# Passing both halves of the transposed probabilities through one value product per key block, in a one-core decoder layer

## Chip, core and metric

One core of one Trainium2 chip runs the whole program. The metric is the device time of one launch in microseconds (us). Five engines matter here: TensorE (PE in the profile; PEld is its weight load), VectorE (DVE), ScalarE (ACT), GpSimd (POOL) and SyncE (SP), which only issues transfers. Each engine takes its instructions strictly in the order of its own queue.

## What is computed

One layer of a decoder trunk on 256 tokens of width 1024, in float32. Three attention mixers run side by side, their outputs are merged by gates, and two layer norms with a feed-forward part follow. Cut to what matters:

```python
proj = x @ w_in                        # queries, keys, values of all three mixers
o_a = dsa_mixer(...)                   # 6 heads, top-64 keys of a learned index, one shared k and v
o_b = dilated_mixer(...)               # 4 slots x 3 window patterns
o_c = moba_mixer(...)                  # 6 heads
...
# in every mixer, at the end:
probs = masked_softmax(logits, mask)
out = jnp.einsum('bqhk,bqkd->bqhd', probs.astype(v.dtype), vsel)
...
merged = (gates[:, :, 0] * (o_a @ w_br_a) + gates[:, :, 1] * (o_b @ w_br_b)
          + gates[:, :, 2] * (o_c @ w_br_c))
x = layer_norm(ALPHA * x + merged @ w_out, ln1_g, ln1_b)
h = jnp.square(jax.nn.relu(x @ w_up)) @ w_down
ple = jax.nn.sigmoid(x @ w_ple_gate) * (p @ w_ple)
x = layer_norm(ALPHA * x + h + ple, ln2_g, ln2_b)
```

With 256 tokens every window and block fits in the sequence, so each mixer becomes dense causal attention with its own mask. The three patterns of a slot of the second mixer share one set of probabilities after they are added up, so 16 times in the program (4 slots, 6 heads of the third mixer, 6 of the first) a 256 x 256 lower triangular matrix of probabilities P is multiplied by 256 x 64 values V.

## The kernel before

Every float32 number that goes into a matrix product is split into a high part that TensorE reads exactly and a low part, the rest. A product of two such numbers then takes three passes, high by high, high by low and low by high (`prod`, L127 to L129), added up in PSUM.

Weights stream in units of up to 128 x 1024 (`Weights`): SP issues the load (L66), ACT writes the high part `whi` (L70), DVE writes the first columns of the low part `wlo` and GpSimd the last ones (L74; of 1024 columns DVE takes 640 and GpSimd 384, of which each column block of 128 belongs to one step of a sum over the width of x). There are five buffers each of the raw weights and of both parts, and a unit's buffers come free only when TensorE, DVE and GpSimd are through with it. Most units feed `gemm`: 24 products of 256 columns, eight blocks of the width times three passes, into one of three PSUM banks named `mm`.

Between these weight products stand the heads. For a head, `logits` (L264) makes the scores into PSUM, DVE adds a bias table T and finds row maxima (L334, L350), ACT takes the exponential (L337, L359) and scales the rows (L326), and `attend` does the rest. P is held as 128 rows by 384 columns: columns 0 to 127 are the first 128 queries by the first 128 keys, columns 128 to 383 are the other 128 queries by all 256 keys. The quarter with early queries and late keys is zero and isn't held.

`attend` transposes the three 128 x 128 pieces on TensorE into the PSUM bank b3 (L303 to L305). ACT copies them as the high part `pth` (L306) and DVE subtracts to get the low part `ptl` (L307). Both are 512 columns wide with a block of 128 zeros in front, set once at the start (L185), so that the late keys can be multiplied over all 256 queries. Four products of 256 columns follow into bank b4 (L310 to L313): the values of each key block by the high and by the low part. The stationary operand holds 64 columns of the values' high part and 64 of their low part, so the upper 64 rows of the result must still be added to the lower 64: ACT copies them down (L315), and DVE adds (L316). For two heads together `pair_out` splits the result (L319, L320) into `op`, which the branch products read later.

In the second mixer (`slots`) GpSimd adds up the three patterns (L361, L362) between the exponential and the scaling. For the first mixer GpSimd also adds the top-k mask `am` to the bias tables well ahead of use (L490, L491, tile `ta`); the tables T come from device memory in three transfers each (L175), since a small product (L374), copied by ACT and written out to `tabd`, makes them at the start.

What the order within each queue is isn't written out: a scheduler with its own model of time orders the instructions of all engines when the program is built, and `tc.high_priority` only moves some of them ahead. So every edit can shift rows far from it.

Of the kernel before, what the change touches and what calls it, by code (L numbers as in the profile page):

```python
# [11 lines left out]
F32 = mybir.dt.float32  # L12
F32R = mybir.dt.float32r
ALU = mybir.AluOpType
# [6 lines left out]
S = 256  # L21
# [67 lines left out]
def hybrid_layer(ctx: ExitStack, tc: tile.TileContext, x0, xn, pT, wqk, wva, wvb, wg, wbc, wba,  # L89
                 wout, wup, wdn, wpg, wple, lnrow, rel, onehot, pick, out):  # L90
    nc = tc.nc
    pe, act, dve, pool = nc.tensor, nc.scalar, nc.vector, nc.gpsimd
# [10 lines left out]
    def turns(ids):  # L103

        while True:
            for i in ids:
                yield banks.tile([128, 512], F32, name=f"b{i}", tag=f"b{i}")

    ps_s, ps_t, ps_v, ps_a = turns((0, 1, 2)), turns((3,)), turns((4,)), turns((0, 1, 3, 2, 4))

    ident = keep.tile([128, 128], F32, name="ident")
# [9 lines left out]
    t = banks.tile([128, 512], F32, name="b4", tag="b4")  # L121
# [22 lines left out]
    p1, k1, kp = (right(n, b) for n, b in (("p1", 1), ("k1", 2), ("kp", 3)))  # L144
# [34 lines left out]
        return t  # L179


    pth = [p1.tile([128, 512], F32R, name=f"pth{i}") for i in range(2)]
    ptl = [p1.tile([128, 512], F32R, name=f"ptl{i}") for i in range(2)]
    for t in pth + ptl:
        pool.memset(t[:, 0:128].bitcast(F32), 0.0)  # L185

    idx = p1.tile([128, 384], F32, name="idx")
    am = p1.tile([128, 384], F32, name="am")
# [81 lines left out]
    V = p1.tile([128, 2, 11, 128], F32R, name="V")  # L270
    iw = p1.tile([128, 2, 8], F32, name="iw")
    op = pm.tile([128, 8, 2, S], F32R, name="op")
# [23 lines left out]
    n_pt = [0]  # L296

    def attend(P, vh, o, h):

        hi, lo = pth[n_pt[0] % 2], ptl[n_pt[0] % 2]  # L300
        n_pt[0] += 1
        t = next(ps_t)
        pe.transpose(t[:, 0:128], P[:, 256:384], ident)  # L303
        pe.transpose(t[:, 128:256], P[:, 0:128], ident)
        pe.transpose(t[:, 256:384], P[:, 128:256], ident)  # L305
        act.copy(hi[:, 128:512], t[:, 0:384])  # L306
        dve.tensor_tensor(lo[:, 128:512], t[:, 0:384], hi[:, 128:512].bitcast(F32),  # L307
                          op=ALU.subtract)
        v = next(ps_v)
        pe.matmul(v[:, 0:S], lhsT=V[:, 0, vh], rhs=hi[:, 256:512], start=True, stop=False)  # L310
        pe.matmul(v[:, 0:S], lhsT=V[:, 0, vh], rhs=lo[:, 256:512], start=False, stop=False)
        pe.matmul(v[:, 0:S], lhsT=V[:, 1, vh], rhs=hi[:, 0:256], start=False, stop=False)
        pe.matmul(v[:, 0:S], lhsT=V[:, 1, vh], rhs=lo[:, 0:256], start=False, stop=True)  # L313
        x = wk2.tile([64, S], F32, name="ov", tag="ov")
        act.copy(x, v[64:128, 0:S])  # L315
        dve.tensor_tensor(o[64 * h:64 * h + 64], v[0:64, 0:S], x, op=ALU.add)  # L316

    def pair_out(o, kt):
        act.copy(op[:, kt, 0], o)  # L319
# [61 lines left out]
    with ExitStack() as begin:  # L381
# [4 lines left out]
        with tc.high_priority(offset=1000):  # L386
# [4 lines left out]
            for k in range(KT):  # L391
                act.copy(xh[:, k], g0[:, k, 0:S])
                for a, b in cut[k]:
                    a = max(a, S)
# [4 lines left out]
        for k in range(KT):  # L399
            for i, (w, x) in enumerate(((sh, xh), (sh, xl), (sl, xh))):  # L400
                for f in range(FIRST):
                    pe.matmul(first[f], lhsT=w[:, k, 128 * f:128 * f + 128], rhs=x[:, k],  # L402
                              start=k == i == 0, stop=k == KT - 1 and i == 2)
        iq = [q_pair(ps, 0.125) for ps in first]
    tp, wk, wk2, sm = (right(n, b) for n, b in (("tp", 3), ("wk", 3), ("wk2", 2), ("sm", 6)))
# [12 lines left out]
    for j in range(4):  # L418
        s = logits(iq[j], kI)
# [21 lines left out]
    def opair():  # L441
        return wk2.tile([128, S], F32, name="o", tag="o")

    for j in range(2):
# [8 lines left out]
        o = opair()  # L453
# [10 lines left out]
    for j in range(3):  # L464
# [3 lines left out]
        s = logits(q, k)  # L468
        o = opair()
# [11 lines left out]
    for j in range(3):  # L481
        q = q_pair(feat(19 + j))
        s = logits(q, kA)
        o = opair()
# [146 lines left out]
    for b in range(2):  # L631
        t = slice(b * 128, (b + 1) * 128)
# [31 lines left out]
    for f in range(32):  # L664
        ps = mmbank(512).rearrange("p (b a t) -> p b a t", b=2, a=2)
        hi, lo = W.get(u_up[f][0])
# [3 lines left out]
        for k in range(KT):  # L670
            pe.matmul(ps[:, :, 0], lhsT=lo[:, cs[k]], rhs=x1[:, :, k, 0], start=False,  # L671
                      stop=k == KT - 1)
# [131 lines left out]
```

## Time and profile before

| what | value |
|---|---|
| runs of the kernel before | 452.64 us median of 3 (451.95 to 453.76) |
| the profiled execution, its time | 451.62 us |
| its span, first to last instruction | 449.8 us |
| granted TensorE clock, mean | 0.996 |
| PE busy | 97% of the span, 2935 products |
| DVE, ACT, POOL busy | 68%, 58%, 23% |
| the stage with the heads | about 17 to 212 us of the span |
| L310 to L313, 16 each | 306, 287, 281, 281 ns mean |

A product's row tells its start and a length that includes the way through the array, so rows of products overlap: the distance from one start to the next is what a product costs the queue. In a timeline row a bracket gives the engine's idle time just before it and what ended it. The profiled execution took 1.8 us more than its span, for what lies around it.

### The profile page before, as it was taken

The page shows a single profiled execution, that of the slowest core. Times are in us where ns is not written, and L with a number is a line of the kernel's source. Part 1 is how long each engine was busy: PE and PEld are TensorE (multiplying, and loading weights), DVE is VectorE, ACT ScalarE, POOL GpSimd, SP SyncE. Part 2 cuts the span into 40 slices and gives each one's busy share as a digit, 9 for nine tenths or more (in the row PEclk, how much of TensorE's full clock was granted, in tenths as well). Part 3 has the DMA queues.
Part 4 walks back from the last instruction along what each step waited for, and adds up shares of the span by engine and source line. Part 5 has one row for each costly group of instructions (what it writes and reads, how often), then busy time and mean ns, then how long its engine had stood idle before and what let it go on. Part 6 is the DMA issues. An engine that isn't in the chain of part 4 may idle for free.

```text
span 449.8 us, 7880 instructions
## 1 busy us (share of the span) xinstructions
PE 436.4 (97%) x2935; PEld 396.1 (88%) x2935; DVE 304.6 (68%) x561; ACT 260.9 (58%) x480; POOL 101.3 (23%) x99
## 2 busy tenths in 40 slices
PE   8999999998999999999999999999999999999993
PEld 8989999988999989999887888888888888888883
DVE  5878977456455677769958689888888644444555
ACT  6765465565787757757415468777777633333400
POOL 2744255478443545400001000000000000000000
PEclk9999999999999999999999999999999999999998
DMA  8883965539534345568952956665666566555202
GB/s 303 306 302 125 287 201 179 154 121 306 178 122 131 117 119 187 142 177 316 296 194 98 330 181 197 198 190 189 191 189 192 170 192 186 189 189 191 68 2 94
DMA packets 27147, 84.30 MB, mean 187 GB/s; under 512 B 2864, under 2 KB 6872, under 8 KB 26724
## 3 DMA queue, kind: packets, MB, share of 16 engines
q1 hardware_dynamic: 25872, 79.54, 54.9%
q10 hardware_dynamic: 1140, 4.19, 2.6%
q8 instruction: 23, 0.38, 0.4%
q14 instruction: 16, 0.13, 0.1%
q0 software_dynamic: 96, 0.06, 0.0%
HBM read 81.88 MB, written 1.90 MB: 186 GB/s over the span
## 4 chain that ended last, share of the span: by engine, by line
PE 87%; DVE 3%; DMA 3%; issue 3%; POOL 1%; ACT 1%; SPq 0%; POOLq 0%; DVEq 0%
PE mm L669 13%; PE mm L127 10%; PE mm L129 10%; PE mm L128 10%; PE b L129 9%; PE b L127 9%; PE b L128 9%; PE mm L671 7%; PE b L264 3%; PE b L402 3%; DMA relt<-in_pick_dram 1%; DMA T<-tabd 1%; DMA pr<-in_pT_dram 1%; DVE st L593 1%; PE b L123 1%
## 5 line engine op out<-in xcount | busy, mean ns | idle before, releaser
L74 DVE TENSOR_TENSOR wlo<-raw,whi 128x1024 fp32r<-128x1024 f32 (+5 forms) x138 | 148.8, 1084 | 72.6 <-ACT whi L70 69.0
L70 ACT CAST whi<-raw 128x1024 fp32r<-128x1024 f32 (+3 forms) x138 | 138.4, 1008 | 90.4 <-PE b L129 45.1
L127 PE MATMUL mm<-xh,whi 128*128 128x256 f32 x336 | 95.0, 283 | 1.0 <-DVE G L244 1.0
L74 POOL TENSOR_TENSOR wlo<-raw,whi 128x384 fp32r<-128x384 f32 (+3 forms) x58 | 77.0, 1334 | 84.2 <-ACT whi L70 76.6
L129 PE MATMUL mm<-xh,wlo 128*128 128x256 f32 x336 | 95.6, 284 | 0.0
L128 PE MATMUL mm<-xl,whi 128*128 128x256 f32 x336 | 94.7, 282 | 0.0
L127 PEld LDWEIGHTS mm<-xh,whi 128*128 128x128 f32 x336 | 63.4, 189 | 1.5 <-DVE G L244 1.2
L669 PE MATMUL mm<-x,whi 128*128 128x512 f32 x256 | 64.1, 392 | 0.0
L129 PEld LDWEIGHTS mm<-xh,wlo 128*128 128x128 f32 x336 | 63.3, 188 | 0.8
L128 PEld LDWEIGHTS mm<-xl,whi 128*128 128x128 f32 x336 | 63.3, 188 | 0.3
L600 POOL TENSOR_TENSOR rs<-rs,half 128x1 f32<-128x1 f32 x4 | 4.1, 1029 | 251.1 <-DVE rs L599 251.1
L669 PEld LDWEIGHTS mm<-x,whi 128*128 128x128 f32 x256 | 46.1, 189 | 8.3
L129 PE MATMUL b<-whi,hT 128*128 128x512 f32 (+1 forms) x150 | 52.6, 350 | 0.0
L128 PE MATMUL b<-wlo,hT 128*128 128x512 f32 (+1 forms) x150 | 52.2, 349 | 0.0
L127 PE MATMUL b<-whi,hT 128*128 128x512 f32 (+1 forms) x150 | 52.0, 348 | 0.0
L671 PEld LDWEIGHTS mm<-x,wlo 128*128 128x128 f32 x256 | 34.9, 190 | 2.5
L671 PE MATMUL mm<-x,wlo 128*128 128x256 f32 x256 | 35.7, 282 | 0.0
L127 PEld LDWEIGHTS b<-whi,hT 128*128 128x128 f32 x150 | 28.2, 188 | 4.1
L128 PEld LDWEIGHTS b<-wlo,hT 128*128 128x128 f32 x150 | 28.2, 188 | 4.1
L129 PEld LDWEIGHTS b<-whi,hT 128*128 128x128 f32 x150 | 28.2, 188 | 3.9
L674 DVE TENSOR_REDUCE r<-mm 128x256 f32<-128x512 f32 x32 | 22.1, 691 | 9.3 <-PE mm L671 9.3
L675 ACT ACTIVATE r<-r 128x256 f32<-128x256 f32 x32 | 13.4, 418 | 13.7 <-DVE r L674 13.7
(167 smaller groups left out, 701.4 us busy)
## 6 DMA issues: line engine op xcount, KB each, us to landing
raw<-in_wup_dram SPq DMA_DIRECT2D x32, 512.0 KB
raw<-in_wdn_dram SPq DMA_DIRECT2D x32, 512.0 KB
raw<-in_wg_dram SPq DMA_DIRECT2D x24, 512.0 KB
raw<-in_wqk_dram SPq DMA_DIRECT2D x18, 512.0 KB
raw<-in_wout_dram SPq DMA_DIRECT2D x8, 512.0 KB
raw<-in_wpg_dram SPq DMA_DIRECT2D x8, 512.0 KB
T<-tabd SPq DMA_DIRECT2D x24, 128.0 KB
G<-in_x_dram SPq DMA_DIRECT2D x7, 384.0 KB
```

The costliest lines, as they stand in the source:

```text
L70: nc.scalar.copy(hi, r)
L74: e.tensor_tensor(lo[:, c], r[:, c], hi[:, c].bitcast(F32), op=ALU.subtract)
L123: pe.transpose(t[:, 0:128], ident, ident)
L127: pe.matmul(ps, lhsT=a[0], rhs=b[0], start=first, stop=False)
L128: pe.matmul(ps, lhsT=a[0], rhs=b[1], start=False, stop=False)
L129: pe.matmul(ps, lhsT=a[1], rhs=b[0], start=False, stop=last)
L264: m = pe.matmul(ss[h][:, QC[b]], lhsT=q[d, x, c], rhs=k[d, y, 0:128 * (b + 1)], start=i == 0, stop=i == 2)
L402: pe.matmul(first[f], lhsT=w[:, k, 128 * f:128 * f + 128], rhs=x[:, k], start=k == i == 0, stop=k == KT - 1 and i == 2)
L669: pe.matmul(ps, lhsT=hi[:, cs[k]], rhs=x1[:, :, k], start=k == 0, stop=False)
L671: pe.matmul(ps[:, :, 0], lhsT=lo[:, cs[k]], rhs=x1[:, :, k, 0], start=False, stop=k == KT - 1)
L674: dve.tensor_reduce(r, ps.rearrange("p b a t -> p b t a"), axis=AX.X, op=ALU.add)
L675: act.activation(r, r, AF.Relu)
```

## The change

The zero block and its four memsets go. The high and the low part of the transposed probabilities lie side by side in one tile, `pts`, as 2 x 384 columns, in P's own order of pieces. Per head there are now two value products instead of four: the early keys by 2 x 256 columns (both parts at once, 512 columns), and the late keys by 2 x 128 columns of the second half of the queries, added onto columns 128 to 255 of each half of the bank. High and low part now stay apart in PSUM, 256 columns each, so the copy of the upper 64 rows is 512 columns wide, the first add is 512 columns wide and a second add of 256 columns joins the two halves.

```diff
-    pth = [p1.tile([128, 512], F32R, name=f"pth{i}") for i in range(2)]
-    ptl = [p1.tile([128, 512], F32R, name=f"ptl{i}") for i in range(2)]
-    for t in pth + ptl:
-        pool.memset(t[:, 0:128].bitcast(F32), 0.0)
+    pts = [p1.tile([128, 2, 384], F32R, name=f"pt{i}") for i in range(2)]
...
-        hi, lo = pth[n_pt[0] % 2], ptl[n_pt[0] % 2]
+        pt = pts[n_pt[0] % 2]
         n_pt[0] += 1
         t = next(ps_t)
-        pe.transpose(t[:, 0:128], P[:, 256:384], ident)
-        pe.transpose(t[:, 128:256], P[:, 0:128], ident)
-        pe.transpose(t[:, 256:384], P[:, 128:256], ident)
-        act.copy(hi[:, 128:512], t[:, 0:384])
-        dve.tensor_tensor(lo[:, 128:512], t[:, 0:384], hi[:, 128:512].bitcast(F32),
-                          op=ALU.subtract)
-        v = next(ps_v)
-        pe.matmul(v[:, 0:S], lhsT=V[:, 0, vh], rhs=hi[:, 256:512], start=True, stop=False)
-        pe.matmul(v[:, 0:S], lhsT=V[:, 0, vh], rhs=lo[:, 256:512], start=False, stop=False)
-        pe.matmul(v[:, 0:S], lhsT=V[:, 1, vh], rhs=hi[:, 0:256], start=False, stop=False)
-        pe.matmul(v[:, 0:S], lhsT=V[:, 1, vh], rhs=lo[:, 0:256], start=False, stop=True)
-        x = wk2.tile([64, S], F32, name="ov", tag="ov")
-        act.copy(x, v[64:128, 0:S])
-        dve.tensor_tensor(o[64 * h:64 * h + 64], v[0:64, 0:S], x, op=ALU.add)
+        for c in range(3):
+            pe.transpose(t[:, 128 * c:128 * c + 128], P[:, 128 * c:128 * c + 128], ident)
+        act.copy(pt[:, 0], t[:, 0:384])
+        dve.tensor_tensor(pt[:, 1], t[:, 0:384], pt[:, 0].bitcast(F32), op=ALU.subtract)
+
+        v = next(ps_v).rearrange("p (a s) -> p a s", a=2)
+        pe.matmul(v, lhsT=V[:, 0, vh], rhs=pt[:, :, 0:256], start=True, stop=False)
+        pe.matmul(v[:, :, 128:256], lhsT=V[:, 1, vh], rhs=pt[:, :, 256:384], start=False,
+                  stop=True)
+        x = wk2.tile([64, 2, S], F32, name="ov", tag="ov")
+        act.copy(x, v[64:128])
+        dve.tensor_tensor(x, v[0:64], x, op=ALU.add)
+        dve.tensor_tensor(o[64 * h:64 * h + 64], x[:, 0], x[:, 1], op=ALU.add)
```

The line numbers of the changed kernel are smaller by 3 behind the first hunk and by 4 behind the second: the transposes are L301, the split L302 and L303, the products L306 and L307, the copy L310, the adds L311 and L312; L361 and L362 become L357 and L358, L490 and L491 become L486 and L487. The scheduler also moves rows. Three places matter.

**Start, GpSimd's queue.** Before, three low parts of 246 columns stand ahead of the loads for the bias table (`oh`, `relt`):

```order
L74 TENSOR_TENSOR wlo<-raw,whi 128x384
L74 TENSOR_TENSOR wlo<-raw,whi 128x246 x3
L370 DMA oh<-in_onehot_dram 36x384
L371 DMA relt<-in_rel_dram 32x24
L372 DMA relt<-in_pick_dram 4x24
L74 TENSOR_TENSOR wlo<-raw,whi 128x246
```

Of the change, the same place:

```order
L74 TENSOR_TENSOR wlo<-raw,whi 128x384
L74 TENSOR_TENSOR wlo<-raw,whi 128x246 x4
L366 DMA oh<-in_onehot_dram 36x384
L367 DMA relt<-in_rel_dram 32x24
L368 DMA relt<-in_pick_dram 4x24
```

The loads moved behind one more low part. On TensorE the product that reads them (L374, now L370) moved back as well, by three products of 328 columns and the first 12 score products.

**Second pair of slots, GpSimd's queue.** `eb` with the lower number is the first head's exponentials, the other the second head's; `ta` are the mask sums, which read the table tile T; `wlo` are low parts of weight units in the order in which TensorE needs them. Before:

```order
L74 TENSOR_TENSOR wlo_1395<-raw_1392,whi_1394 128x384
L361 TENSOR_TENSOR eb_1243<-eb_1243 128x384
L490 TENSOR_TENSOR ta_2177<-T_2173,am_124 128x128
L491 TENSOR_TENSOR ta_2177<-T_2173,am_124 128x256
L490 TENSOR_TENSOR ta_2263<-T_2173,am_124 128x128
L491 TENSOR_TENSOR ta_2263<-T_2173,am_124 128x256
L362 TENSOR_TENSOR eb_1243<-eb_1243 128x384
L361 TENSOR_TENSOR eb_1244<-eb_1244 128x384
L74 TENSOR_TENSOR wlo_1414<-raw_1411,whi_1413 128x384
```

Of the change:

```order
L357 TENSOR_TENSOR eb_1235<-eb_1235 128x384
L358 TENSOR_TENSOR eb_1235<-eb_1235 128x384
L486 TENSOR_TENSOR ta_2161<-T_2157,am_118 128x128
L487 TENSOR_TENSOR ta_2161<-T_2157,am_118 128x256
L357 TENSOR_TENSOR eb_1236<-eb_1236 128x384
L486 TENSOR_TENSOR ta_2246<-T_2157,am_118 128x128
L487 TENSOR_TENSOR ta_2246<-T_2157,am_118 128x256
L486 TENSOR_TENSOR ta_2383<-T_2157,am_118 128x128
L487 TENSOR_TENSOR ta_2383<-T_2157,am_118 128x256
L74 TENSOR_TENSOR wlo_1385<-raw_1382,whi_1384 128x384
L74 TENSOR_TENSOR wlo_1404<-raw_1401,whi_1403 128x384
L358 TENSOR_TENSOR eb_1236<-eb_1236 128x384
```

Both sums of the first head now stand ahead of the first `ta`, and the low part of the next unit (1395 before, 1385 now, the same weights) moved from the front to behind three pairs of `ta`.

**The same place on TensorE.** `mm_1472` before and `mm_1462` now is the sum over that unit; b3 is the bank of the transposes. Before, behind the first 18 of its 24 products:

```order
L127 MATMUL mm_1472<-xh_112,whi_1394 128x256
L128 MATMUL mm_1472<-xl_113,whi_1394 128x256
L303 MATMUL b3_1312<-ident_75,eb_1243 128x128
L304 MATMUL b3_1312<-ident_75,eb_1243 128x128
L305 MATMUL b3_1312<-ident_75,eb_1243 128x128
L129 MATMUL mm_1472<-xh_112,wlo_1395 128x256
```

Of the change, from the sum's first row:

```order
L127 MATMUL mm_1462<-xh_112,whi_1384 128x256
L128 MATMUL mm_1462<-xl_113,whi_1384 128x256
L129 MATMUL mm_1462<-xh_112,wlo_1385 128x256
L127 MATMUL mm_1462<-xh_112,whi_1384 128x256
L128 MATMUL mm_1462<-xl_113,whi_1384 128x256
L301 MATMUL b3_1304<-ident_75,eb_1235 128x128
L129 MATMUL mm_1462<-xh_112,wlo_1385 128x256
L127 MATMUL mm_1462<-xh_112,whi_1384 128x256
L301 MATMUL b3_1304<-ident_75,eb_1235 128x128 x2
L128 MATMUL mm_1462<-xl_113,whi_1384 128x256
L129 MATMUL mm_1462<-xh_112,wlo_1385 128x256
```

The first transpose moved from behind 20 products of the sum to behind 5, the other two to behind 7. Behind the rows shown the sum goes on in its plain order, high, high, low.

## The prediction, made before the changed kernel ran

> **What bounds the kernel.** I read the page first, then TensorE's timeline for the places where it stands still, then the queues of the engines that it waits for there.
>
> ```profile
> PE 436.4 (97%) x2935; PEld 396.1 (88%) x2935; DVE 304.6 (68%) x561; ACT 260.9 (58%) x480; POOL 101.3 (23%) x99
> ```
>
> TensorE is busy 97% of the span, and nearly all the rest is the start and the end. So time can only go where TensorE gets fewer columns or stands still less. Between the start and the first layer norm its timeline has four real stops. Each is shown with the product in front of it where that gives the length:
>
> ```profile
> 25.88 0.48 PE L374 MATMUL b<-oh,relt 36*24 36x384 f32 x1 [0.40 <-DMA relt<-in_pick_dram]
> ...
> 96.79 0.27 PE L128 MATMUL mm<-xl,whi 128*128 128x256 f32 x1
> 98.09 0.30 PE L303 MATMUL b<-ident,eb 128*128 128x128 f32 x1 [1.03 <-POOL eb L362]
> ...
> 104.66 0.28 PE L128 MATMUL mm<-xl,whi 128*128 128x256 f32 x1
> 106.09 0.30 PE L303 MATMUL b<-ident,eb 128*128 128x128 f32 x1 [1.16 <-POOL wlo L74]
> ...
> 160.75 0.28 PE L129 MATMUL mm<-op,wlo 128*128 128x256 f32 x1
> 162.03 0.39 PE L127 MATMUL mm<-xh,whi 128*128 128x256 f32 x1 [1.01 <-DVE G L244]
> ```
>
> From start to start, less the 0.12 that the product in front costs, the stops last 1.18, 1.31 and 1.16 us, some 0.15 more than the brackets say. So the first one, 0.40 in its bracket, is taken as 0.55. None of them is in the value products themselves. The change touches this list in two ways: by the columns of the heads, and by the scheduler's new order around the first three stops.
>
> **The products.** What a product costs the queue is its distance to the next:
>
> ```profile
> 102.41 0.28 PE L312 MATMUL b<-pth,V 128*128 128x256 f32 x1
> 102.53 0.28 PE L313 MATMUL b<-ptl,V 128*128 128x256 f32 x1
> ```
>
> That is 0.12 for one of 256 columns. The feed-forward stage has eight in a row, and by luck in just the shapes of the change, since its moving operand is also 2 x 128 or 4 x 128 columns with a stride (chain of work: start, length, what):
>
> ```profile
> 265.07 0.95 PE mm L671 x8
> 266.02 1.84 PE mm L669 x8
> ```
>
> 0.95 / 8 = 0.119 for 256 strided columns, 1.84 / 8 = 0.230 for 512. Per head four products, 4 x 0.119 = 0.476, become 0.230 + 0.119 = 0.349. Times 16 heads this is **-2.03 us**. All of it lies in TensorE's own queue, so it counts in full wherever TensorE doesn't wait.
>
> [...]
>
> **What the heads get in return.** ACT's copy and DVE's first add grow to 512 columns, and DVE gets a second add. Rows by source line, minimum, median and maximum in ns; L622 and L623 read 512 columns from PSUM, L245 adds 256 columns that all lie in SBUF:
>
> ```profile
> L315 ACT COPY ov<-b x16: 369/370/372, 73.6 to 197.7; 64x256 f32<-64x256 f32 x16
> L316 DVE TENSOR_TENSOR o<-b,ov x16: 406/417/419, 74.6 to 198.1; 64x256 f32<-64x256 f32 x16
> L622 ACT CAST x<-b x4: 579/589/604, 238.5 to 243.5; 128x512 fp32r<-128x512 f32 x4
> L623 DVE TENSOR_TENSOR x<-b,x x4: 678/680/692, 239.2 to 244.2; 128x512 fp32r<-128x512 f32 x4
> L245 DVE TENSOR_TENSOR G<-G x8: 407/426/1244, 163.6 to 203.8; 128x256 f32<-128x256 f32 x8
> ```
>
> ACT pays 0.589 - 0.370 = 0.22 per head, DVE 0.680 - 0.417 + 0.426 = 0.69, so 11 us of DVE in all. I cost it at nothing, because the stage where it is densest has room (columns: stretch, length, then busy time and instructions of PE, PEld, DVE, ACT, POOL):
>
> ```profile
> 180.00:212.00 32.00, 32.00 (x267) 31.39 (x266) 24.93 (x46) 21.79 (x43) 5.15 (x4) 1.00 0.66 214
> ```
>
> Six of the sixteen heads at most lie there, 4.1 us against 7 us of idle DVE. Bank b4 is held longer (0.589 + 0.680 instead of 0.370 + 0.417), but the nearest two heads' products are still 24 weight products, 24 x 0.12 = 2.9 us, apart. Behind the longer adds on DVE's queue stand the next head's low part and the low parts of weights, whose units are some 2.8 us of TensorE each and converted several units ahead. If that cover were gone, 16 x (0.22 + 0.69) = 14.6 us would be the price; below nothing there is no gain, as nothing gets shorter.
>
> **The start.** GpSimd issues the table's loads behind one more low part, and TensorE's product on them stands later:
>
> ```profile
> 19.94 5.80 DMA relt<-in_pick_dram
> ```
>
> ```profile
> 20.48 1.70 POOL L74 TENSOR_TENSOR wlo<-raw,whi 128x246 fp32r<-128x246 f32 x2
> ```
>
> The loads go out 1.70 / 2 = 0.85 later and land at 25.74 + 0.85 = 26.6. TensorE passes three products of 328 columns (0.15 each by columns) and 12 score products (0.88, a row of the next part) first, so it comes to the table product 1.3 later than 25.3 (25.88 less 0.55), and no longer waits: **-0.55**. Bounds are 0 and -0.55. The copy of the table to device memory starts 1 to 2 us later behind ACT's new order; what covers this is that the load of a weight unit no longer stands behind the tables on SP's queue. The mask's memset of 0.41 us now stands ahead of the identity, in place of two smaller ones; I take **+0.1**, between 0 and 0.41.
>
> **The second pair of slots** is the open part. I measure from the last score products of the slots, since every chain here starts from them. The rows are the first product of the unit that TensorE comes to next, two of the chain of work for what score products and transposes cost, and GpSimd's queue:
>
> ```profile
> 94.54 0.28 PE L127 MATMUL mm<-xh,whi 128*128 128x256 f32 x1
> ```
>
> ```profile
> 76.17 0.88 PE b L264 x12
> ...
> 106.39 0.11 PE b L304
> ```
>
> ```profile
> 87.47 1.66 POOL L74 TENSOR_TENSOR wlo<-raw,whi 128x384 fp32r<-128x384 f32 x1 [2.87 <-ACT whi L70]
> ...
> 92.84 0.94 POOL L490 TENSOR_TENSOR ta<-T,am 128x128 f32<-128x128 f32 x1 [2.54 <-DMA T<-tabd]
> ...
> 96.14 1.01 POOL L362 TENSOR_TENSOR eb<-eb 128x384 f32<-128x384 f32 x1
> 97.11 1.00 POOL L361 TENSOR_TENSOR eb<-eb 128x384 f32<-128x384 f32 x1
> 98.06 1.03 POOL L74 TENSOR_TENSOR wlo<-raw,whi 128x384 fp32r<-128x384 f32 x1
> 99.03 0.47 POOL L490 TENSOR_TENSOR ta<-T,am 128x128 f32<-128x128 f32 x1
> ...
> 100.15 1.61 POOL L74 TENSOR_TENSOR wlo<-raw,whi 128x384 fp32r<-128x384 f32 x1
> ```
>
> Before, GpSimd waits for T until 92.84 with the first head's second sum behind it, and this makes both stops at 98.09 and 106.09. In the new order both sums of the first head come ahead of that wait, so the first transposes find their rows ready: -1.18. But the low part of the next unit now stands behind the wait and three pairs of `ta`. On the clock of before, T lands at 92.84 still. Then two pairs take 96.14 - 92.84 = 3.30, the sum between them 98.06 - 97.11 = 0.95, the third pair 100.15 - 99.03 = 1.12, the low part 99.03 - 98.06 = 0.97: done at 99.18. TensorE needs GpSimd's columns first in the sixth low product of the unit. It starts the unit at 94.54 + 3 x 0.12 = 94.90 (three more products stand behind the scores than before), and 17 products of 0.119 and three transposes of 0.11 lie ahead: 94.90 + 2.02 + 0.33 = 97.25. So a **new stop of about 2.0** comes, on a low weight product, while both old ones go, since the second head's sum follows 1.94 behind the low part and TensorE then has 7 + 21 products and a head's two to do, 3.7. Net -1.18 - 1.31 + 2.0 = **-0.5**. Bounds: with every GpSimd step at the slowest rate shown, 1.65 for a pair or a sum of 384 and 1.66 for the low part, it ends at 92.84 + 3 x 1.65 + 1.65 + 1.66 = 101.1, a stop of 3.9; if T lands two us earlier there is none. I take the uncrowded one, because DVE has no long run at that time.
>
> SP now issues all tables ahead of two weight loads, which so wait for this GpSimd chain; their units come some four units of 24 products, about 11 us, later on TensorE.
>
> **The stop at 162.03** stays.
>
> ```profile
> 160.56 0.82 DVE L74 TENSOR_TENSOR wlo<-raw,whi 128x640 fp32r<-128x640 f32 x1 [2.44 <-ACT whi L70]
> 161.30 0.68 DVE L244 SCALAR_TENSOR_TENSOR G<-G,mm 128x512 f32<-128x512 f32 x1
> ```
>
> A unit's buffer comes free when TensorE ends a query sum; ACT's and DVE's conversion and then L244 follow, which frees the bank. The order keeps these rows, but TensorE has 0.35 + 3 x 0.11 + 6 x 0.119 = 1.39 to do meanwhile, before 10 x 0.119 + 3 x 0.11 = 1.52: **+0.1**. At the first layer norm rows are swapped too:
>
> ```profile
> 243.63 0.50 PE L127 MATMUL b<-whi,x 128*128 128x512 f32 x1 [0.24 <-ACT x L622]
> ```
>
> One such wait may go, or one DVE row of 0.68 may come in between; I take 0.
>
> **The sum**: -2.03 - 0.55 + 0.1 - 0.5 + 0.1 = -2.9 from the profiled execution's 451.62, so 448.7. The median of the runs is 1.0 above that execution; on its scale I say 449.8.
>
> **Rivals.**
> - *The low part comes in time.* If T lands early, the new stop goes and the change gains 2.0 more: 447.8. For it: fewer loads stand between the tables. Against it: the table that waits is still the fourth of its row. Chance 0.12.
> - *GpSimd is crowded.* The stop is 3.9: 451.7. For it: the low part at 87.47 took 1.66 and the one at 98.06 only 1.03. Chance 0.20. [...]
> - *DVE becomes the bound: slower.* A head's first product used to need the high part alone, now both parts. Where DVE's queue is so late that the low part isn't there after the shortest distance from transposes to products, 24 products or 2.9 us, the added 0.91 per head shows. In half of the heads this is 8 x 0.91 = 7.3, so 457. For it: DVE at 78% near the end. Against it: the two steps need 0.589 + 0.680 at most. Chance 0.08.
> - *The wide product saves nothing* (its reads stride over two halves): 451.8. L669 speaks against it. Chance 0.10.
>
> The forecast keeps 0.50. **Range** 447.3 to 453.0: from the early table with 0.5 of small stops less to the crowded case with one more stop of 1.2, as the trace has them. A measurement here can tell about 0.5%, 2.3 us. Faster than 450.4 are the first rival and three quarters of the forecast, 0.50; slower only DVE, 0.08; within, 0.42.
>
> **What would show it.** Value products of 0.23 and 0.12; no wait before the table product; no wait before the slots' transposes, but one of about 2 before a low weight product, ended by GpSimd's L74; the bank's stop still near 1.2. Stops before value products, ended by DVE, would prove me wrong, as would several new stops elsewhere from the new order.

## The result, and the profile after

The changed kernel took **458.5 us** (median of 4 runs, 456.77 to 459.7) against 452.29 for the kernel before on the same chip (median of 4): a ratio of **1.0143, 95% interval 1.0119 to 1.0168**. It is 6.2 us slower; the prediction said 449.8, between 447.3 and 453.0. The profiled execution took 456.77 us with a span of 455.0, 5.15 and 5.2 more than before.

The first line of the changed kernel's page, as before: busy time, share of the span and instructions of each engine.

```profile
PE 437.3 (96%) x2903; PEld 395.9 (87%) x2903; DVE 312.1 (69%) x577; ACT 264.2 (58%) x480; POOL 100.9 (22%) x95
```

32 products fewer, as the change says, and yet TensorE's busy time is 0.9 us longer, and its mean granted clock is 0.986 where before it was 0.996. So some products run slower. First, what the change promised. TensorE's timeline at the first head, and the view of the first value product's line, with its 16 instructions and, behind "sat idle", what TensorE waited for ahead of them (the view of the second, L307, has nothing there either):

```profile
74.87 0.28 PE L129 MATMUL mm<-xh,wlo 128*128 128x256 f32 x1
74.99 0.40 PE L306 MATMUL b<-pt,V 128*128 128x512 f32 x1
75.23 0.28 PE L307 MATMUL b<-pt,V 128*128 128x256 f32 x1
75.35 0.49 PE L301 MATMUL b<-ident,eb 128*128 128x128 f32 x3
```

```profile
L306 PE MATMUL b<-pt,V x16: 388/396/403, 75.0 to 199.0; 128*128 128x512 f32 x16
its engine sat idle before it (us, times) until:
```

75.35 - 74.99 = 0.36 for this head, and 5.65 us from start to start over all 16, 0.353 each, where the prediction had 0.349; and nothing stands behind the colon: no head's products wait for the wider evacuation. Now the stops. These are TensorE's rows at which it stood still for over half a microsecond between the table product and the first layer norm:

```profile
67.46 0.39 PE L127 MATMUL mm<-xh,whi 128*128 128x256 f32 x1 [0.89 <-DVE k L216]
...
99.55 0.39 PE L129 MATMUL mm<-xh,wlo 128*128 128x256 f32 x1 [2.37 <-POOL wlo L74]
...
157.81 0.39 PE L127 MATMUL mm<-xh,whi 128*128 128x256 f32 x1 [0.48 <-ACT G L228]
...
163.44 0.39 PE L127 MATMUL mm<-xh,whi 128*128 128x256 f32 x1 [1.12 <-DVE G L241]
...
210.86 0.28 PE L129 MATMUL mm<-op,wlo 128*128 128x256 f32 x1
213.57 0.80 PE L127 MATMUL b<-whi,q 128*128 128x512 f32 x1 [2.43 <-ACT q L556]
...
217.81 0.50 PE L129 MATMUL b<-whi,q 128*128 128x512 f32 x1 [0.57 <-DVE q L557]
```

Each is some 0.15 longer than its bracket, as before: 1.05, 2.52, 0.64, 1.29, 2.59 and 0.73 us. The wait before the table product and the two before the slots' transposes are gone. The stop at 67.46 stands ahead of the first value products (74.99), so it can't come of their evacuation. The stop at 99.55 is the one that the prediction saw coming, on a low weight product and behind the same queue:

```profile
92.08 0.83 POOL L486 TENSOR_TENSOR ta<-T,am 128x128 f32<-128x128 f32 x1 [1.83 <-DMA T<-tabd]
...
93.57 1.61 POOL L357 TENSOR_TENSOR eb<-eb 128x384 f32<-128x384 f32 x1
...
96.83 1.03 POOL L486 TENSOR_TENSOR ta<-T,am 128x128 f32<-128x128 f32 x1
97.83 0.72 POOL L487 TENSOR_TENSOR ta<-T,am 128x256 f32<-128x256 f32 x1
98.51 1.96 POOL L74 TENSOR_TENSOR wlo<-raw,whi 128x384 fp32r<-128x384 f32 x2
```

T lands 0.76 us earlier than the forecast had it, at 92.08, but two pairs of `ta`, the sum between them, the third pair and the low part take 7.4 us instead of 6.3 (the sum alone 1.56 from its start to the next, instead of 0.95).

The one at 213.57, at the first product of the output projection, it did not see. ScalarE's timeline there shows what q waited for, first of the changed kernel, then of the kernel before:

```profile
202.39 1.05 ACT L70 CAST whi<-raw 128x1024 fp32r<-128x1024 f32 x1
...
209.31 1.05 ACT L70 CAST hT<-raw 128x1024 fp32r<-128x1024 f32 x1 [5.87 <-DMA raw<-in_wout_dram]
210.26 2.94 ACT L70 CAST whi<-raw 128x1024 fp32r<-128x1024 f32 x3
213.10 0.72 ACT L556 ACTIVATE q<-G 128x256 fp32r<-128x256 f32 x2
```

```profile
205.86 1.05 ACT L70 CAST whi<-raw 128x1024 fp32r<-128x1024 f32 x1 [1.11 <-PE mm L128]
206.81 0.72 ACT L560 ACTIVATE q<-G 128x256 fp32r<-128x256 f32 x2
207.91 1.05 ACT L70 CAST hT<-raw 128x1024 fp32r<-128x1024 f32 x1 [0.38 <-DMA raw<-in_wout_dram]
```

The cast into `hT` belongs to the second half of the output projection's weights, which are written into `hT` and so need no free buffer of their own. Before, it stood behind the first merge's casts to q; now it stands ahead of three weight casts and of q, and waits 5.87 us for its load. No other row of ScalarE stands in those 5.87 us, and VectorE waits 3.32 us for the cast, until 210.39, to make the low part of `hT`, with the merge's G (L553, 211.53) behind that. So the merges' results are stuck behind a load that nobody needs yet.

The stops do not explain all of the time. The windows around the two long ones (columns: stretch, length, busy time and instructions of PE, PEld, DVE, ACT, POOL, granted clock, DMA share, GB/s) have the other half:

```profile
98.00:100.00 2.00, 0.45 (x3) 0.45 (x4) 0.02 (x1) 0.00 (x0) 2.00 (x3) 1.00 0.08 5
100.00:102.00 2.00, 2.00 (x15) 2.00 (x14) 0.00 (x0) 0.53 (x2) 2.00 (x3) 0.73 0.71 204
102.00:104.00 2.00, 2.00 (x12) 2.00 (x11) 0.00 (x0) 0.54 (x2) 2.00 (x3) 0.50 0.92 320
104.00:106.00 2.00, 2.00 (x17) 1.96 (x17) 0.69 (x1) 1.13 (x2) 0.32 (x1) 0.92 0.95 347
...
212.00:214.00 2.00, 0.43 (x1) 0.43 (x2) 2.00 (x4) 2.00 (x5) 0.00 (x0) 0.89 0.57 143
214.00:216.00 2.00, 2.00 (x6) 1.52 (x6) 2.00 (x3) 1.51 (x2) 0.00 (x0) 0.50 0.74 203
216.00:218.00 2.00, 1.43 (x5) 0.72 (x4) 2.00 (x4) 1.23 (x4) 0.00 (x0) 0.76 0.71 236
```

Behind each of them the granted clock falls to 0.50: 2.00 x (0.27 + 0.50 + 0.08) = 1.7 us of TensorE's work lost behind the first, 2.00 x (0.11 + 0.50 + 0.24) = 1.7 behind the second. None of the three long stops of the kernel before, 1.31 us at most, was followed by anything of the kind: in the windows behind them, 99.4 to 102.8, 106.2 to 109.6 and 163.4 to 167, the clock is 1.00.

The account, after less before, in us:

| where | term |
|---|---|
| value products, 16 x (0.353 - 0.476) | -2.0 |
| table product's wait gone | -0.55 |
| stop at 67.46, new | +1.05 |
| second pair of slots: 2.52 in place of 1.18 and 1.31 | +0.03 |
| clock behind it | +1.7 |
| stop at 157.81, new | +0.64 |
| gate's bank: 1.29 in place of 1.16 | +0.13 |
| output projection: 2.59 and 0.73, new | +3.3 |
| clock behind it | +1.7 |
| first layer norm: one stop of 0.45 in place of four of 1.3 together | -0.8 |
| sum, to be held against 5.2 | +5.2 |

TensorE's last product starts 4.9 us later than before (446.89 against 441.99), and 0.3 lies behind it, so the account closes to within 0.3.

### The profile page after: what moved, and what is told of

It reads as the page before. It is cut to its first block, busy times and chain, and to the rows that moved or that the text cites. A ratio compares the mean times of both kernels' runs of the same rounds, so it can differ in the third digit from the quotient of the medians.

```text
span 455.0 us, 7811 instructions
## 1 busy us (share of the span) xinstructions
PE 437.3 (96%) x2903; PEld 395.9 (87%) x2903; DVE 312.1 (69%) x577; ACT 264.2 (58%) x480; POOL 100.9 (22%) x95
## 4 chain that ended last, share of the span: by engine, by line
PE 84%; issue 3%; DVE 3%; DMA 3%; ACT 3%; POOL 2%; POOLq 0%; SPq 0%; DVEq 0%; ACTq 0%
PE mm L665 13%; PE mm L127 10%; PE mm L129 10%; PE mm L128 9%; PE b L129 9%; PE b L127 9%; PE b L128 9%; PE mm L667 7%; PE b L261 3%; PE b L398 3%; DMA raw<-in_wout_dram 2%; DVE wlo L74 1%; PE b L301 1%; DMA T<-tabd 1%; ACT whi L70 1%
## 5 line engine op out<-in xcount | busy, mean ns | idle before, releaser
L127 PE MATMUL mm<-xh,whi 128*128 128x256 f32 x336 | 97.0, 289 | 2.5 <-DVE G L241 1.1
L128 PE MATMUL mm<-xl,whi 128*128 128x256 f32 x336 | 95.8, 285 | 0.0
L74 POOL TENSOR_TENSOR wlo<-raw,whi 128x384 fp32r<-128x384 f32 (+3 forms) x58 | 75.4, 1308 | 82.2 <-ACT whi L70 69.6
```

Source lines behind the costliest of these rows:

```text
L74: e.tensor_tensor(lo[:, c], r[:, c], hi[:, c].bitcast(F32), op=ALU.subtract)
L127: pe.matmul(ps, lhsT=a[0], rhs=b[0], start=first, stop=False)
L128: pe.matmul(ps, lhsT=a[0], rhs=b[1], start=False, stop=False)
```

## The experiments

**Theory.** The saving on the products is real. The loss is two long stops that the new order makes, on GpSimd's queue near 99 us and on ScalarE's near 210, each with a stretch of half clock behind it. **Rivals**: A, the stops count alone and the clock has no part; B, the wider evacuation is the cost; C, the late load only moves the wait; D, the products save nothing.

Ratios are to the kernel before, with 95% intervals; 0.001 is 0.45 us. The rows of an experiment carry the line numbers of its own kernel. In the edits `tc.issue_after(x)` makes the scheduler queue what stands under it behind the instruction x.

### e1, e2, e3: each stop taken away, and both

e1 holds GpSimd's sums of table and mask behind the last low part issued ahead of the last six heads:

```diff
-            e.tensor_tensor(lo[:, c], r[:, c], hi[:, c].bitcast(F32), op=ALU.subtract)
+            m = e.tensor_tensor(lo[:, c], r[:, c], hi[:, c].bitcast(F32), op=ALU.subtract)
+            if e is nc.gpsimd:
+                self.low = m.ins
...
+    low = W.low
     for j in range(3):
         q = q_pair(feat(19 + j))
...
-            pool.tensor_tensor(ta[:, 0:128], T[:, n % 3, 128:256], am[:, 0:128], op=ALU.add)
-            pool.tensor_tensor(ta[:, 128:384], T[:, n % 3], am[:, 128:384], op=ALU.add)
+            with tc.issue_after(low):
+                pool.tensor_tensor(ta[:, 0:128], T[:, n % 3, 128:256], am[:, 0:128], op=ALU.add)
+                pool.tensor_tensor(ta[:, 128:384], T[:, n % 3], am[:, 128:384], op=ALU.add)
```

> The changed kernel, with GpSimd's sums of tables and mask (ta) queued behind the last low weight part that was issued ahead of the last six heads, so that no ta stands ahead of wlo near 99 us; nothing else in the queues of that stage moves. Theory (the loss is two long stops that the new order makes, each with a stretch of half clock behind it): the stop of 2.52 us at 99.55 goes and the granted clock stays 1.00 there, which gives back 2.5 + 1.7, so 458.5 - 4.2 = 454.3 us; the stop of 2.59 at 213.6 stays with its dip. Rival A (stops alone count, the clock has no part): 458.5 - 2.5 = 456.0. Rival B (the wider evacuation on VectorE and ScalarE is the cost): 458 to 459, unchanged.

e2 holds the casts into `hT` behind the first merge's casts; the loads are not held:

```diff
-        nc.scalar.copy(hi, r)
+        with ExitStack() as held:
+            if self.late is not None:
+                held.enter_context(self.tc.issue_after(self.late))
+            nc.scalar.copy(hi, r)
...
-            act.mul(m[:, 0], g[:, f], 0.5)
+            i = act.mul(m[:, 0], g[:, f], 0.5).ins
+            cast.append(i)
...
+    W.late = cast[1]
     for k in range(4):
         outp.step(k)
+    W.late = None
```

> The changed kernel, with ScalarE's casts of the second half of the output projection (written into hT) queued behind the first merge's casts of q, so that the cast that waits for its load no longer stands ahead of them. Theory: the stop of 2.59 us at 213.6 goes or falls under 1, the small one of 0.73 behind it too, and the clock stays 1.00; 458.5 - 2.6 - 1.7 = 454.2 us, or down to 453.5 with the small one; the stop at 99.55 stays. Rival A (stops alone): 455.9. Rival C (the load itself is late, and the projection would wait for it at a later place): under 1 us is gained, 457.5 or more, with a stop at the products of that unit. Rival B (evacuation): unchanged.

e3 has both.

> Both holds together: sums later and casts first. Theory: both long stops and both stretches of half clock go, 458.5 - 4.2 - 4.2 = 450.1 us, which is faster than the kernel before by about 2 us, since the products' columns are saved as forecast. Rival A (stops alone): 453.4. Rival B (evacuation): 458. Rival D (the products save nothing): about 452.3, the time before, with no long stop left.

| run | median us | before | ratio | less than the change (1.0143) by |
|---|---|---|---|---|
| e1 | 454.08 | 451.52 | 1.0059 [1.0035, 1.0084] | 3.8 us |
| e2 | 452.17 | 451.52 | 1.0012 [0.9999, 1.0025] | 5.9 us |
| e3 | 448.89 | 451.52 | 0.9945 [0.9928, 0.9962] | 9.0 us |

The theory had 4.2, 4.2 to 5.0 and 8.4; rival A 2.5, 2.6 and 5.1. e2's and e3's times part the two; e1's, with some 1.6 us of uncertainty from both intervals, does not by itself. Its trace does: counted in order of start, the 501st product with a weight begins at 93.97 us in the changed kernel and at 94.54 in e1, the 651st at 118.54 and at 114.99. The stage between is 4.1 us shorter, which is the theory's 4.2 and not A's 2.5. e1's merges also stood longer than the change's, 3.25 and 2.26 us in the profiled execution, where 2.59 and 0.73 had been expected to stay. Rival B falls with e3: every head still has the wide evacuation there. Rival C falls with e2. ScalarE's queue there, and the stage of the second pair of slots in e1 as one window:

```profile
208.51 0.72 ACT L560 ACTIVATE q<-G 128x256 fp32r<-128x256 f32 x2
209.98 1.05 ACT L74 CAST hT<-raw 128x1024 fp32r<-128x1024 f32 x1 [0.74 <-DMA raw<-in_wout_dram]
```

```profile
96.00:104.00 8.00, 8.00 (x69) 7.95 (x69) 5.45 (x7) 4.02 (x8) 6.13 (x5) 1.00 0.77 258
```

In e2 q is cast at 208.51 instead of 213.10, and the cast that follows finds its load almost there. In e1 TensorE is busy for all of the 8 us from 96 to 104, at full clock.

### e4, e11: how long a stop may be

In e4 and e11 the kernel before gets stops of a set length in its last projection: a small product, a chain of ScalarE casts on its result, a small product on theirs, and the next step held behind it.

```diff
+    STOPS = {2: 2, 5: 3, 8: 4, 11: 5, 14: 6, 17: 7, 20: 4, 23: 5}
     for k in range(26):
-        down.step(k)
+        with ExitStack() as held:
+            if z_mm is not None:
+                held.enter_context(tc.issue_after(z_mm))
+            down.step(k)
+        if k not in STOPS:
+            continue
...
+        tc.keep_in_program_order(pe.matmul(a, lhsT=hi[:, 0:128], rhs=hi, start=True, stop=True))
+        act.copy(z, a)
+        for _ in range(STOPS[k] - 1):
+            act.copy(z, z.bitcast(F32))
+        z_mm = pe.matmul(b, lhsT=hi[:, 0:128], rhs=z, start=True, stop=True).ins
```

> The kernel before, with eight stops of TensorE put into the last projection, between steps 2, 5, 8, 11, 14, 17, 20 and 23 and the next: a small product, a chain of 2, 3, 4, 5, 6, 7, 4 and 5 ScalarE casts of 256 columns on its result, a small product on theirs, and every product of the next step behind it. Some 0.8 + 0.36 us per cast: stops of about 1.5, 1.9, 2.2, 2.6, 3.0, 3.3, 2.2 and 2.6 us, 19.4 in all. Theory (a stop of 2.5 us or more is followed by a stretch of half clock, one of 1.3 isn't): the granted clock falls to 0.5 for about 3.4 us behind the stops of 5, 6 and 7 casts and not behind the one of 2, so about 452.3 + 19.4 + 4 x 1.7 = 478.5 us; where the bound lies between 1.3 and 2.5 is open. Rival A (the clock does not fall with stops of this length): 1.00 behind all of them, 471.7 us.

One run, 490.41 us. The stops were longer than I worked out, 1.88, 2.32, 2.76, 3.20, 3.64, 4.06, 2.76 and 3.19 us, 23.8 in all. The one of 1.88 was not followed by half clock, the other seven were: with the 16 small products at 0.12 the sum is 451.5 + 23.8 + 1.9 + 7 x 1.7 = 489.1, and without the clock, as rival A has it, 477.2. The first two stops, by their rows and by windows of 3.4 us:

```profile
364.12 0.39 PE L714 MATMUL mm<-z,hT 128*128 128x256 f32 x1 [1.72 <-ACT z L713]
375.21 0.39 PE L714 MATMUL mm<-z,hT 128*128 128x256 f32 x1 [2.16 <-ACT z L713]
```

```profile
362.20:365.60 3.40, 1.68 (x9) 1.25 (x8) 1.23 (x1) 1.72 (x3) 0.00 (x0) 1.00 0.49 161
365.60:369.00 3.40, 3.40 (x19) 2.89 (x18) 0.55 (x1) 1.05 (x1) 0.00 (x0) 1.00 0.55 154
372.40:375.80 3.40, 1.24 (x9) 0.99 (x8) 1.30 (x2) 2.12 (x4) 0.00 (x0) 1.00 0.54 174
375.80:379.20 3.40, 3.40 (x11) 2.61 (x10) 0.00 (x0) 0.00 (x0) 0.00 (x0) 0.50 0.49 154
```

More than the lengths, the beginnings said something: the seven stretches of half clock began at 375.8, 389.5, 403.1, 416.8, 430.4, 444.1 and 457.7, all on one grid of 3.41 us, while the stops ended 0.3 to 1.3 us ahead of them. So I formed a second theory, by the share of a grid step that is idle, and e11 puts in eleven stops of one length (three casts each).

> The kernel before with eleven stops of one length, about 2.32 us (three casts in the chain, as the second stop of e4), behind steps 1, 3, 5, 8, 10, 12, 15, 17, 19, 22 and 24 of the last projection. In e4 every stretch of half clock began on one grid of 3.41 us (375.8, 389.46, 403.1, 416.76, 430.4, 444.07, 457.72) and lasted one step of it; a stop of 1.88 inside one step had none, and in e1 a stop of 3.25 split evenly by such a step had none either. Theory G (the clock halves for the next step of the grid when about 2 us or more of one step are idle; between 1.88 and 2.05): stops of 2.32 that fall inside a step are followed by a stretch, those of which less than 1.9 us lies in one step are not, so about half of the eleven, and each decided by its place. Rival H (the length of the stop alone decides, from about 2): all eleven.

One run, 496.96 us. Ten of the stops were 2.32 us long, one came out at 4.61. Two of the ten had no half clock behind them. Their rows are alike; here one without and one with, and the windows laid on the grid, whose steps are read from where the granted clock changes:

```profile
392.52 0.39 PE L714 MATMUL mm<-z,hT 128*128 128x256 f32 x1 [2.16 <-ACT z L713]
400.78 0.39 PE L714 MATMUL mm<-z,hT 128*128 128x256 f32 x1 [2.16 <-ACT z L713]
```

```profile
388.23:391.64 3.41, 2.13 (x13) 1.69 (x11) 1.51 (x2) 1.63 (x4) 0.00 (x0) 1.00 0.60 181
391.64:395.05 3.41, 2.53 (x12) 2.13 (x13) 0.94 (x1) 0.79 (x2) 0.00 (x0) 1.00 0.62 203
398.47:401.88 3.41, 1.25 (x7) 0.97 (x6) 1.23 (x1) 2.12 (x4) 0.00 (x0) 1.00 0.50 156
401.88:405.29 3.41, 3.41 (x12) 2.85 (x12) 0.00 (x0) 0.00 (x0) 0.00 (x0) 0.50 0.49 151
```

The stop that ends at 392.52 lies across a step of the grid, 1.44 us in one window and 0.88 in the next, and the clock stays at 1.00. The one that ends at 400.78 lies in one window with 2.31, and the next window is at 0.50. The other stop without half clock, ending at 423.24, is split in the same way, 1.44 and 0.88. So rival H (length alone) falls, and theory G holds for these stops, but with less idle time than I put it: 9 of 11 had half clock behind them, because in three stops 1.89 to 1.91 us inside one step were enough. One of these three:

```profile
377.99:381.40 3.41, 1.50 (x7) 1.28 (x8) 1.23 (x1) 1.80 (x4) 0.00 (x0) 1.00 0.64 167
381.40:384.81 3.41, 3.41 (x13) 2.94 (x12) 0.00 (x0) 0.40 (x1) 0.00 (x0) 0.50 0.37 141
```

e4's stop of 1.88, which lies whole inside one step, was not enough. By TensorE's busy time in the windows the two are further apart, since a product's row ends some 0.15 us after the moment from which I count a stop: 3.41 - 1.50 = 1.91 us idle here, 3.40 - 1.68 = 1.72 in e4. What an amount between these two does, neither run shows.

### e5, e10, e9: what the change is worth with the same holds

e5 is the kernel before with both holds and without the change.

> The kernel before with the same two holds as e3 (sums of tables and mask later, casts of hT behind the first merge's casts), without the change. This parts what the change saves from what the holds save. Theory (the products are worth 2.0 us and the table's wait 0.55, whatever the order): before's stops of 1.18 and 1.31 at the second pair of slots go, so about 2.5 us or a ratio of 0.9945 to the kernel before, and e3 would then have to be lower than this by what its own stops differ: if e3 (0.9945) is no better than this, the change is worth nothing by itself and the theory falls. If the holds save before only the sum of the two stops' brackets less what comes next, 1 to 2 us (0.996 to 0.998), e3 is ahead by 0.5 to 1.5. Rival D (the products save nothing, e3's gain is all the holds'): 0.9945 or less.

449.05 us, 0.9945 [0.9927, 0.9963]: the same as e3. By what I had written, the change would then be worth nothing by itself. The spans of the profiled executions said otherwise, 446.0 us for e3 against 447.5 for e5, so both ran again, as e9 and e10, side by side.

> e3 once more, on one chip with e5 once more: what the change is worth where both kernels have the same two holds. The profiled executions differ by 1.5 us (446.0 against 447.5 of span; 1.01 of it ahead of the output projection, where the change keeps a stop of 1.06 at 68 us that e5 hasn't), the medians by 0.2. By the trace: a ratio to the kernel before that is 0.002 to 0.0035 lower than that of e10. By the first medians: the same ratio, 0.9945.

> e5 once more, beside e9: about 0.9945 of the kernel before, with stops of 1.16 at the gate's bank and 1.28 in all at the first layer norm and none at the second pair of slots.

e9: 448.0 us, 0.9928 [0.9910, 0.9946], span 447.3. e10: 449.12 us, 0.9952 [0.9935, 0.9969], span 448.5. So the change is ahead by 0.0024 in one pair and 0 in the other, about 0.5 us between the means of the pairs, and by 1.5 and 1.2 in the spans. Its size stays open, between 0 and 1.5 us by these figures. That it is less than the 2.0 of the products is likely, but not shown: the intervals of e9 and e10 overlap, and their far ends are 2.7 us apart. The spans are no firmer, since each execution has stops of its own. e10 has one of 1.29 us at the second pair of slots, where its expectation had none and where e5, the same kernel, has none; e9 has one of 1.02 at 215.57, of which e3 has 0.2. The row of e10's:

```profile
107.62 0.36 PE L316 MATMUL b<-pth,V 128*128 128x256 f32 x1 [1.13 <-DVE o L322]
```

The traces name part of what eats the rest: with the holds the change still stops for 1.05 us at 68, which e5 and e10 don't (the row is e3's):

```profile
68.04 0.39 PE L133 MATMUL mm<-xh,whi 128*128 128x256 f32 x1 [0.90 <-DVE k L222]
```

Both pairs are the fastest versions here. The holds are worth 2.2 to 2.5 us to the kernel before as well.

### e6, e8: is it the columns?

On e3. e6 gives the second product the zero block's columns back, so its first 128 query rows get a wrong addend:

```diff
-        pe.matmul(v[:, :, 128:256], lhsT=V[:, 1, vh], rhs=pt[:, :, 256:384], start=False,
-                  stop=True)
+        pe.matmul(v, lhsT=V[:, 1, vh], rhs=pt[:, :, 128:384], start=False, stop=True)
```

> e3 with the second value product of each head also 512 columns wide (it runs over the columns of both key blocks from 128 on, so the first 128 query rows get a wrong addend): the columns of the zero block are back, in one product. Theory (a product costs its columns, 0.230 for 512 and 0.119 for 256, all in TensorE's queue): + 16 x 0.111 = 1.8 us on e3, ratio 0.9985 to the kernel before. Rival D (columns of these products don't matter): as e3, 0.9945.

449.75 us, 0.9959 [0.9944, 0.9974], an interval that doesn't part it from e3. In the trace the products of the 16 heads take 7.46 us from start to start, e3's 5.68, so 1.78 more, just the theory's term; the output projection begins 1.73 us later than in e3 (208.49 against 206.76). The columns are paid in full up to there, and rival D falls; the medians, 0.9 us apart, say only that something of it is left at the end.

e8 splits the two products into four without the zero block:

```diff
-        pe.matmul(v, lhsT=V[:, 0, vh], rhs=pt[:, :, 0:256], start=True, stop=False)
-        pe.matmul(v[:, :, 128:256], lhsT=V[:, 1, vh], rhs=pt[:, :, 256:384], start=False,
-                  stop=True)
+        for a in range(2):
+            pe.matmul(v[:, a], lhsT=V[:, 0, vh], rhs=pt[:, a, 0:256], start=True, stop=False)
+            pe.matmul(v[:, a, 128:256], lhsT=V[:, 1, vh], rhs=pt[:, a, 256:384], start=False,
+                      stop=True)
```

> e3 with the two wide products per head split again into four, of 256, 128, 256 and 128 columns: the same columns without the zero block, one product per part and block. Theory (the saving is the zero block's columns and not the width): 2 x (0.119 + 0.06 to 0.073) = 0.36 to 0.38 per head instead of 0.349, so 0.1 to 0.6 us more than e3. Rival E (fewer and wider products are what saves): 0.476 per head as before, 2.0 us more.

One run, 450.96 us, no interval. In the trace the products of the 16 heads take 5.99 us from start to start, 0.3 more than e3's 5.68 and inside the theory's 0.1 to 0.6; by rival E they would take 7.6. What saves is that the zero block isn't multiplied, and hardly that the products are fewer and wider. By its time alone the run, 3.15 us above e3's profiled execution, would fit rival E. The largest part of that is a stop ahead of the next projection, which in e3 lasts 0.2 us, and which waits for a weight cast:

```profile
217.39 0.50 PE L133 MATMUL mm<-whi,ph 128*128 128x512 f32 x1 [1.72 <-ACT whi L74]
```

e9, which is e3 once more, has 1.02 us of that stop too, so in part it belongs to the execution. Some 1.2 us more, spread over the heads, I cannot place.

### e7: the evacuation

e3 with the second add of each head done twice.

```diff
-        dve.tensor_tensor(o[64 * h:64 * h + 64], x[:, 0], x[:, 1], op=ALU.add)
+        for _ in range(2):
+            dve.tensor_tensor(o[64 * h:64 * h + 64], x[:, 0], x[:, 1], op=ALU.add)
```

> e3 with the new second add of each head (L312 of the changed kernel, 0.42 us on VectorE) done twice: 16 x 0.42 = 6.7 us more of VectorE. Theory (the wider evacuation lies beside TensorE): as e3, within 0.5 us. Rival B (the evacuation is on the path): 3.4 us more if half of the heads show it, 6.7 if all do.

449.95 us, 0.9963 [0.9951, 0.9975], 0.8 us above e3 and 1.6 above e9, for 6.7 us more of VectorE. So the evacuation is nearly hidden, but not for nothing, as I had said. TensorE's timeline shows where it comes through, at the merges behind the last pair of heads:

```profile
200.78 0.67 PE L133 MATMUL mm<-op,whi 128*128 128x256 f32 x3 [0.35 <-ACT op L322]
...
202.54 0.39 PE L134 MATMUL mm<-op,whi 128*128 128x256 f32 x1 [0.37 <-DVE op L323]
```

## Why the prediction was wrong

- **The products**, -2.03: right in mechanism and size. 0.353 us per head, and e6 gives the saving back by the same columns.
- **The start**, -0.55: right; the wait is gone. The margin was thin: the forecast had the loads and TensorE both at 26.6; in the changed kernel the last load, issued at 21.09 and 5.9 us on its way, is there at 27.0, and TensorE comes at 27.28.
- **The second pair of slots**, -0.5: the mechanism was right, the stop comes on the low part behind the three pairs of `ta`. It was mis-sized, 2.52 instead of 2.0 (inside the bounds 0 to 3.9), because GpSimd's steps were slower than the rows that I took them from (the sum at 93.57 took 1.61 us, beside two low parts of VectorE that ran from 93.46 to 95.85; the one of before at 97.11 took 1.00, with VectorE idle), and the term lacked the clock behind it, 1.7. What I called -0.5 was +1.7.
- **The list of places** is the step that failed. I wrote that the new order matters "around the first three stops" and looked for it there, at the gate's bank and at the layer norm. Its dearest effect lies at the merges, where TensorE had no stop before: the order put a cast that waits for a load ahead of q on ScalarE. The new place of the cast was there to be read in the two orders, ahead of any run, though not that it would wait 5.87 us; I read the queues only where the trace of before had a stop. It costs 3.3 of stops and 1.7 of clock, 5.0 in all, of the 8.1 that lie between the forecast's -2.9 and the +5.2 of the profiled executions. The prediction named "several new stops elsewhere from the new order" as a sign of being wrong, but gave them no price: the 1.2 us that the range kept for one more stop was a quarter of this.
- **A stop was priced at its own length.** Before, the longest of the stops shown was 1.31 us, and the clock behind it stayed at 1.00. Together with the points above the sum would have been -2.9 + 2.2 + 5.0 + 1.05 + 0.64 - 0.8 = +5.2.
- **The rivals.** GpSimd crowded came nearest of them, in part: the stop was longer than forecast, yet far from its 3.9. VectorE as the bound, the one on the slow side, did not happen, since no value product waits. That the wide product saves nothing is refuted. The evacuation costed at nothing is off by a little: doubling one part of it cost 0.8 to 1.6 us in e7. Part of the changed kernel's stop of 0.64 at 157.81 may be its price as well, since the wider copy stands ahead of the wait in ScalarE's queue; e1 and e3, with the same evacuation, don't have that stop.
- **The changed kernel's own gain** is what e3 and e9 show, 0.5 to 0.7% below the kernel before, holds included. On the 452.64 that the forecast started from this is 449.4 to 450.1. That the forecast's 449.8 lies there is luck, since most of that gain is the holds': the change's part is 0 to 1.5 us.

Not tried: why the load for `hT` took 6.27 us, from 202.96 to 209.23. The 1 MB load of X is issued beside it on another queue at 202.41, and before it was issued at 199.76. Whether the one slows the other is not shown.

## What to carry to other kernels

When a scheduler orders the work, a change of a few instructions in one stage can reorder a queue far from it: compare the new order of every queue with the old one along the whole program, and look above all for an instruction that waits for a load and now stands ahead of one that TensorE needs. Price a stop of TensorE with the clock behind it: here it cost its length up to 1.88 us, and above that 1.7 more wherever TensorE was idle for 1.9 us or more of one 3.41 us step between changes of the clock. Before crediting a change with a gain, put whatever else was mended on the old kernel as well.

## What the hardware showed that I had not expected

The granted clock changed on a grid. In the changed kernel, e1, e4 and e11, every stretch of half clock that followed a stop lasted 3.41 us, and those of one run began whole steps of 3.41 us apart: at 100.92 and 213.56 in the changed kernel, 33 steps. In the step just ahead of each, TensorE was idle for 2.04 and 2.40 us in the changed kernel, 2.10 in e1, 2.10 to 3.06 in e4 and 1.9 to 3.1 in e11; no stretch followed a step with 1.72 in e4 or 1.64 in e1. A longer stop passed without one: in e1 the output projection waits 3.25 us, until 210.00, and then 2.26, until 214.24, and only the second has half clock behind it. The windows on the grid of that run:

```profile
204.95:208.36 3.41, 1.96 (x17) 1.76 (x15) 1.54 (x2) 2.62 (x3) 0.00 (x0) 1.00 0.15 60
208.36:211.77 3.41, 1.77 (x8) 1.42 (x8) 3.41 (x5) 3.05 (x6) 0.00 (x0) 1.00 0.56 157
211.77:215.19 3.42, 1.31 (x6) 0.81 (x5) 3.42 (x7) 2.60 (x4) 0.00 (x0) 1.00 0.75 261
215.19:218.60 3.41, 3.41 (x10) 2.66 (x9) 3.41 (x6) 1.85 (x4) 0.00 (x0) 0.50 0.75 210
```

The stop of 3.25 is split 1.61 and 1.64 between the first two windows. Counted from the start of the span, the grid isn't at the same place in every run: e4 and e11 have one source up to the last projection, and two of their stretches begin at 375.8 and at 381.4, 5.6 apart and so not a whole number of steps. By my estimate the same stop may thus cost 1.7 us more in one run than in the next; no run shows it for one kernel. Whether that is behind the 2.9 us over which the changed kernel's four runs spread is open. The shortest and the longest have the same mean granted clock, 0.986, in which one stretch is worth 0.004, which speaks against it; but the clock also falls to 0.50 at the program's end, where TensorE has nothing left to do (in the changed kernel's profile it is 0.54 from 449 to 450 and 0.50 from there to 455), and a step more or less of that is worth as much.
